# An absolute-sum normalization: summing and scaling of the first tile divided between two engines, 7 rows and 5

## The chip, the core and the metric

The kernel runs on one core of a Trainium2 chip. The engines that matter here are VectorE (DVE in the profile), ScalarE (ACT), SyncE (SP, which only issues transfers) and the core's 16 DMA engines, which move data between the chip's main memory (HBM) and the on-chip memory that the engines work on. The metric is device time in microseconds; the time of a kernel is the median of its runs.

## The reference

```python
# x: (32, 512, 1024) float32
def reference(x):
    sums = np.sum(np.abs(x), axis=-1, keepdims=True)
    return (x / (sums + 1e-8)).astype(np.float32)
```

Each of the 16384 rows of 1024 numbers is divided by the sum of its absolute values. 67.11 MB are read and 67.11 MB are written.

## The kernel before

The input is seen as 16384 rows. 128 partitions take part throughout, and each partition has 128 rows of its own. A tile is `[128, R, 1024]` with `R = 12` rows for each partition, so one tile is 6144 KB, and 49152 bytes of it lie in each partition. There are 11 tiles: the list `rows` holds ten times 12 and at the end 8. The first two tiles and the last one, of 8 rows, together make up the "head" of 32 rows a partition; `piece` says which rows of memory a tile covers. Its rows lie together in memory for each partition.

For each tile `i` in order the program does this:

- SP issues the load into `x_tile` (L78 before, L91 after the change). The pool `sbuf` has four buffers, so the first four loads are issued at once, and the load of tile `i + 4` is held on SP until the store of tile `i` has landed.
- `normalize` puts on DVE a sum of absolute values over all rows of the tile (`tensor_reduce`, L51, into `s`), an addition of 1e-8 (L58), a reciprocal (L60, into `inv`), and a product with `inv` in place for the first `kv` rows (L61). The remaining rows are scaled on ACT, one instruction a row (`activation` with `Copy` and a scale, L68). `kv` is `k - k // 3`: 8 of 12 rows are on DVE and 4 on ACT; in the last tile 6 and 2.
- ACT issues the store (L80), after its own rows and DVE's product are done.

All instructions of an engine run in the order in which the program puts them there (`manual_schedule`). So the store of a tile stands on ACT behind that tile's row copies, and the sum of the next tile stands on DVE behind the product of this one. Loads and stores use two separate queues, one fed by SP (q1 in the profile) and one fed by ACT (q10), on the same 16 DMA engines. One transfer is spread over all 16 engines, 8 partitions on each.

Of the kernel before, what the change touches and what calls it, by code (L numbers as in the profile page):

```python
# [1 line left out]

# [4 lines left out]

FP32 = mybir.dt.float32
EPS = 1e-8


@with_exitstack
def kernel(
    ctx: ExitStack,
    tc: tile.TileContext,
    x: bass.AP,
    out: bass.AP,
):
    nc = tc.nc
    P = nc.NUM_PARTITIONS  # L20

    x_flat = x.flatten_outer_dims()
    out_flat = out.flatten_outer_dims()
    n, d = x_flat.shape

    R = 12
    BUFS = 4  # L30
    HEAD = 32
    per_partition = n // P
    assert n % P == 0 and (per_partition - HEAD) % R == 0
    rows = [R] * ((per_partition - HEAD) // R + 2) + [HEAD - 2 * R]

    def piece(flat, i):
        head = flat[: P * HEAD, :].rearrange("(p r) d -> p r d", p=P)
        if i < 2:
            return head[:, R * i : R * (i + 1), :]
        if i == len(rows) - 1:  # L40
            return head[:, 2 * R :, :]
        a = P * (HEAD + R * (i - 2))
        return flat[a : a + P * R, :].rearrange("(p r) d -> p r d", p=P)

    sbuf = ctx.enter_context(tc.tile_pool(name="sbuf", bufs=BUFS))
    stats = ctx.enter_context(tc.tile_pool(name="stats", bufs=4))

    def normalize(x_tile, r0, k, kv):

        s = stats.tile([P, R], FP32)  # L50
        nc.vector.tensor_reduce(  # L51
            out=s[:, :k],
            in_=x_tile[:, r0 : r0 + k, :],
            axis=mybir.AxisListType.X,
            op=mybir.AluOpType.add,
            apply_absolute_value=True,
        )
        nc.vector.tensor_scalar_add(out=s[:, :k], in0=s[:, :k], scalar1=EPS)  # L58
        inv = stats.tile([P, R], FP32)
        nc.vector.reciprocal(out=inv[:, :k], in_=s[:, :k])  # L60
        nc.vector.tensor_mul(  # L61
            out=x_tile[:, r0 : r0 + kv, :],
            in0=x_tile[:, r0 : r0 + kv, :],
            in1=inv[:, :kv].unsqueeze(2).to_broadcast([P, kv, d]),
        )
        for r in range(kv, k):
            row = x_tile[:, r0 + r, :]
            nc.scalar.activation(  # L68
                out=row,
                in_=row,  # L70
                func=mybir.ActivationFunctionType.Copy,
                scale=inv[:, r : r + 1],
            )

    with tc.manual_schedule():
        for i, k in enumerate(rows):
            x_tile = sbuf.tile([P, R, d], FP32)
            nc.sync.dma_start(out=x_tile[:, :k, :], in_=piece(x_flat, i))  # L78
            normalize(x_tile, 0, k, k - k // 3)
            nc.scalar.dma_start(out=piece(out_flat, i), in_=x_tile[:, :k, :])  # L80


# [1 line left out]
_INS = ['x']  # L84
_OUTS = [((32, 512, 1024), 'float32')]


# [23 lines left out]
```

## Time and profile before

| | us |
|---|---|
| median of 7 runs | 317.62 |
| lowest and highest run | 317.0, 318.92 |
| the profiled run's own time | 318.92 |
| its span, first to last instruction | 317.3 |
| DVE busy | 235.8 (74%) |
| ACT busy | 46.1 (15%) |
| loads, q1 | 67.11 MB, 49.6% of 16 engines' span |
| stores, q10 | 67.11 MB, 48.9% |

The span is the time between the first and the last instruction of the profiled execution; the run's own time is 1.6 us longer. Busy time is the time in which an engine ran instructions. The share of a DMA queue is the time that its packets took, as a part of the span of all 16 DMA engines. A packet is here the part of a transfer that one engine moves in one piece: a partition's 49152 bytes, or 32768 bytes in the last tile. The records of the packets have for each its queue, start, duration and size. Times in the timeline count from the span's start.

### The profile page before, as it was taken

To read this page: it belongs to the slowest core of one execution; us is meant where nothing else is said; L and a number is where in the kernel's file an instruction comes from. 1 tells how busy PE (TensorE), PEld (TensorE's weight loads), DVE (VectorE), ACT (ScalarE), POOL (GpSimd) and SP (SyncE) were. 2 spreads that over 40 slices of the span, in tenths; PEclk is the share of its full clock that TensorE was granted. 3 is DMA by queue.
4 is the path that set the end of the run, shared out by engine and by line. 5 is a ranking of instruction groups with operands and counts; after the bars stand their busy time and mean duration, and the time that the engine had idled before them with its cause. 6 is when DMAs were issued, how large, how long until landed. Compare 5 with 4: busy or idle time off the path is not lost.

```text
span 317.3 us, 205 instructions
## 1 busy us (share of the span) xinstructions
DVE 235.8 (74%) x44; ACT 46.1 (15%) x43; POOL 0.2 (0%) x4
## 2 busy tenths in 40 slices
DVE  0079999999999599659928990997399469979400
ACT  0010402205005004000500140031005000502000
POOL 0000000000000000000000000000000000000000
DMA  8999999999999999999999999999999999999994
GB/s 335 459 397 483 409 384 403 421 471 403 465 421 403 483 403 428 465 403 452 434 403 471 409 440 446 409 465 421 403 466 421 428 432 459 403 463 421 415 426 202
DMA packets 3170, 134.23 MB, mean 423 GB/s; under 512 B 353, under 2 KB 353, under 8 KB 353
## 3 DMA queue, kind: packets, MB, share of 16 engines
q1 hardware_dynamic: 1584, 67.11, 49.6%
q10 hardware_dynamic: 1584, 67.11, 48.9%
q14 instruction: 2, 0.01, 0.0%
HBM read 67.11 MB, written 67.11 MB: 423 GB/s over the span
## 4 chain that ended last, share of the span: by engine, by line
another core or an unknown queue 36%; DMA 31%; DVE 26%; SPq 0%; issue 0%; DVEq 0%; ACTq 0%
DMA out_dram<-x_tile 16%; DMA x_tile<-in_x_dram 15%; DVE s L51 15%; DVE x_tile L61 10%; SPq L78 0%; DVE inv L60 0%; DVE s L58 0%; DVEq L60 0%; ACTq L80 0%
## 5 line engine op out<-in xcount | busy, mean ns | idle before, releaser
L51 DVE TENSOR_REDUCE s<-x_tile 128x12 f32<-128x12288 f32 (+1 forms) x11 | 138.2, 12562 | 59.6 <-DMA x_tile<-in_x_dram 59.6
L61 DVE TENSOR_TENSOR x_tile<-x_tile,inv 128x8192 f32<-128x8192 f32 (+1 forms) x11 | 93.5, 8498 | 0.4
L68 ACT ACTIVATE x_tile<-x_tile,inv 128x1024 f32<-128x1024 f32 x42 | 44.8, 1137 | 228.8 <-DVE inv L60 228.8
L68 ACT ACT_TABLE_LOAD x1 | 1.3, 1283 | 17.7 <-DMA x_tile<-in_x_dram 17.7
L60 DVE RECIPROCAL inv<-s 128x12 f32<-128x12 f32 (+1 forms) x11 | 2.5, 226 | 0.9
L58 DVE TENSOR_SCALAR s<-s 128x12 f32<-128x12 f32 (+1 forms) x11 | 1.9, 173 | 0.4
L95 POOL MEMSET const-bfloat16-1.0<- 128x1 bf16 x1 | 0.1, 101 | 0.0
L95 POOL MEMSET const-uint8-127<- 128x1 uint8 x1 | 0.1, 101 | 0.0
L95 POOL MEMSET const-float32-0.0<- 128x1 f32 x1 | 0.1, 98 | 0.2 <-issue 0.2
L95 POOL MEMSET const-float32-1.0<- 128x1 f32 x1 | 0.1, 98 | 0.0
## 6 DMA issues: line engine op xcount, KB each, us to landing
x_tile<-in_x_dram SPq DMA_DIRECT2D x10, 6144.0 KB, 34.2
out_dram<-x_tile ACTq DMA_DIRECT2D x10, 6144.0 KB, 52.5
x_tile<-in_x_dram SPq DMA_DIRECT2D x1, 4096.0 KB, 31.1
out_dram<-x_tile ACTq DMA_DIRECT2D x1, 4096.0 KB, 19.1
```

Source lines behind the costliest of these rows:

```text
L51: nc.vector.tensor_reduce(out=s[:, :k], in_=x_tile[:, r0 : r0 + k, :], axis=mybir.AxisListType.X, op=mybir.AluOpType.add, apply_absolute_v ...
L58: nc.vector.tensor_scalar_add(out=s[:, :k], in0=s[:, :k], scalar1=EPS)
L60: nc.vector.reciprocal(out=inv[:, :k], in_=s[:, :k])
L61: nc.vector.tensor_mul(out=x_tile[:, r0 : r0 + kv, :], in0=x_tile[:, r0 : r0 + kv, :], in1=inv[:, :kv].unsqueeze(2).to_broadcast([P, kv, d]),)
L68: nc.scalar.activation(out=row, in_=row, func=mybir.ActivationFunctionType.Copy, scale=inv[:, r : r + 1],)
L95: nc = _bacc.Bacc("TRN2", target_bir_lowering=False, num_devices=1)
```

## The change

`normalize` gets a further argument, `ks`: the sum on DVE covers the first `ks` rows, and ACT sums each of the other rows with an `activation` of the function `Abs` that also accumulates along the row into `s` (L65). What that instruction writes as its ordinary output goes to `junk`, a buffer in PSUM (the accumulation memory) that nobody reads. The addition of 1e-8 (now L71) then waits for DVE's sum and for ACT's. For tile 0 both `ks` and `kv` are 7 (of 12 rows), so that DVE sums and scales 7 rows and ACT sums and scales 5. For all other tiles `ks = k` and `kv = k - k // 3`, as before. The argument `r0`, which was always 0, is dropped. In the order of instructions nothing else moves, except that ACT's load of its function table stands ahead of the first wait for tile 0 instead of behind it.

```diff
+    psum = ctx.enter_context(
+        tc.tile_pool(name="psum", bufs=1, space=bass.MemoryType.PSUM)
+    )
+    junk = psum.tile([P, d], FP32)
+
-    def normalize(x_tile, r0, k, kv):
+    def normalize(x_tile, k, ks, kv):
         s = stats.tile([P, R], FP32)
         nc.vector.tensor_reduce(
-            out=s[:, :k],
-            in_=x_tile[:, r0 : r0 + k, :],
+            out=s[:, :ks],
+            in_=x_tile[:, :ks, :],
             axis=mybir.AxisListType.X,
             op=mybir.AluOpType.add,
             apply_absolute_value=True,
         )
+        for r in range(ks, k):
+            nc.scalar.activation(
+                out=junk[:, :],
+                in_=x_tile[:, r, :],
+                func=mybir.ActivationFunctionType.Abs,
+                accum_out=s[:, r : r + 1],
+            )
         nc.vector.tensor_scalar_add(out=s[:, :k], in0=s[:, :k], scalar1=EPS)
...
             nc.sync.dma_start(out=x_tile[:, :k, :], in_=piece(x_flat, i))
-            normalize(x_tile, 0, k, k - k // 3)
+            if i == 0:
+                normalize(x_tile, k, k * 7 // 12, k * 7 // 12)
+            else:
+                normalize(x_tile, k, k, k - k // 3)
             nc.scalar.dma_start(out=piece(out_flat, i), in_=x_tile[:, :k, :])
```

More of the change, by code (lines that the diff above doesn't have):

```diff
@@ L61, in normalize @@
         nc.vector.tensor_mul(
-            out=x_tile[:, r0 : r0 + kv, :],
-            in0=x_tile[:, r0 : r0 + kv, :],
+            out=x_tile[:, :kv, :],
+            in0=x_tile[:, :kv, :],
             in1=inv[:, :kv].unsqueeze(2).to_broadcast([P, kv, d]),
@@ L66, in normalize @@
         for r in range(kv, k):
-            row = x_tile[:, r0 + r, :]
+            row = x_tile[:, r, :]
             nc.scalar.activation(
```

## The prediction

> **What bounds the kernel now.** I read the page first, for the share of each resource.
>
> ```profile
> span 317.3 us, 205 instructions
> DVE 235.8 (74%) x44; ACT 46.1 (15%) x43; POOL 0.2 (0%) x4
> DMA  8999999999999999999999999999999999999994
> q1 hardware_dynamic: 1584, 67.11, 49.6%
> q10 hardware_dynamic: 1584, 67.11, 48.9%
> ```
>
> No engine is full, but the 16 DMA engines are: loads (q1) and stores (q10) together take 98.5% of the span, and only the first and the last slice lack a 9. Next I read busy time by stretches (columns: us, DVE, ACT, POOL, clock, DMA share, GB/s), cut where the first store begins and where the loads end.
>
> ```profile
> 1.70:42.00 40.30, 24.22 (x5) 5.55 (x5) 0.00 (x0) 1.00 1.01 429
> 46.00:276.00 230.00, 188.81 (x36) 38.39 (x36) 0.00 (x0) 1.00 1.00 432
> 281.00:302.00 21.00, 15.62 (x4) 2.19 (x2) 0.00 (x0) 1.00 1.02 440
> 302.00:313.00 11.00, 0.00 (x0) 0.00 (x0) 0.00 (x0) 1.00 0.92 399
> 313.00:317.30 4.30, 0.00 (x0) 0.00 (x0) 0.00 (x0) 1.00 0.05 23
> ```
>
> Loads alone, loads with stores, and stores alone all move 429 to 440 GB/s at a full DMA. The mixture is neither dearer nor cheaper, so an earlier mixture wins no bandwidth. The packet records say why: a 49152-byte packet takes 1.815 us on its engine in either queue, and a 32768-byte packet of the last tile 1.213 us. Each engine carries 8 packets of each transfer: 2 x (80 x 1.815 + 8 x 1.213) = 309.8 us. The records run from 1.73 to 315.86, 314.1 us. So 4.3 us at most is not plain transfer: 0.7 in the first packets, 1.2 where the first store joins, the rest on one late engine. Of the 16, 14 begin the last store at 303.2 to 304.1 and end by 313.8, one ends at 314.4, and the latest begins at 306.2 and ends at 315.9.
>
> The third view is the timeline, at both ends (start, duration, engine, line).
>
> ```profile
> 17.67 12.95 DVE L51 TENSOR_REDUCE s<-x_tile 128x12 f32<-128x12288 f32 x1 [17.67 <-DMA x_tile<-in_x_dram]
> 39.91 0.38 ACTq L80 DMA_DIRECT2D out_dram<-x_tile  x1
> 109.69 12.95 DVE L51 TENSOR_REDUCE s<-x_tile 128x12 f32<-128x12288 f32 x1 [3.70 <-DMA x_tile<-in_x_dram]
> 281.18 8.69 DVE L51 TENSOR_REDUCE s<-x_tile 128x8 f32<-128x8192 f32 x1 [2.03 <-DMA x_tile<-in_x_dram]
> 297.06 0.34 ACTq L80 DMA_DIRECT2D out_dram<-x_tile  x1
> ```
>
> The first store is issued at 39.91; from 109.69 on DVE waits for loads; the last load lands at 281.16 and the last store is issued 15.9 us later, at 297.06. The engines then still work on older stores until 303.2 or later. That cover, 6.1 us, is the number on which the change turns.
>
> **The change, part by part.** Tile 0 on DVE before: from 17.67 to 39.82, 22.15 us. After: its sum has 7 rows instead of 12. The forms of L51 give 12950 ns for 12 rows and 8686 for 8, so 1066 a row and 7.62 us for 7, a saving of 5.33. The product has 7 rows instead of 8: L61 gives 8692 ns for 8 rows and 6558 for 6, so 7.63 us, a saving of 1.07. In all 6.40 us.
>
> ACT gets five summing instructions. No row of before has one that accumulates. From below, the copies of L68 take 1137 ns and follow each other at 1067 (4.27 us for four), so five take 5.4 us. From above, I let each cost twice the copy, 2.27 us, for the wait of each on the one before and for bringing out the sum: 11.4 us. I take 1.3 us each, near the copy, the same 1024 elements in and out: 6.5 us, under DVE's 7.62. If that cover is gone, the add at L71, and the reciprocal and product queued behind it on DVE, start 3.8 us later, and the first store comes 2.6 us earlier instead of 6.4. ACT's fifth copy is hidden: 5 x 1.07 = 5.3 us beside a product of 7.63. The function-table load (1.28 us), which waited for the first load, no longer does and runs under it.
>
> One rule speaks against the change. The Trainium skill, "ScalarE: Activation LUTs", section "Rules for kernel authors", sends sums and products to VectorE rather than ScalarE; the trace has 1066 ns a row for DVE's sum and 1067 between ACT's copies, so a second engine is worth a second engine here. By the rule tile 0 would stay at 22.15 us, by the rows it falls to 15.75.
>
> So the first store is issued at about 33.5 instead of 39.9. DVE then finds tile 1 in place: loads alone need 8 x 1.815 = 14.5 us each, so the second lands at 17.65 + 14.5 = 32.2, before DVE is free at 33.4. Stores 1 to 8 stay queued ahead of need: before, store 0's packets begin at 45.2 and each store takes 29 us beside loads, while stores 1 and 2 are issued at 62.0 and 84.0. The fifth load, which SP holds until store 0 has landed, is issued some 6 us sooner, but queues behind the fourth.
>
> Now what the 6.4 us buy. The two queues alternate packet by packet. With the stores starting D earlier, D worth of load packets is pushed into the shared stretch, where each also waits for a store packet. So every later load, the last one too, lands D later, with D as much more store data done. The work left is the same. D is 6.4 us, in whole packets 5.4 (three) or 7.3 (four). The last landing moves to 287.6, and the last store's issue to 303.5 (302.5 to 304.3). DVE's wait before the last tile stays, as tile 9 moves along.
>
> The older stores still end at 303.2 to 304.1 on most engines, so the cover of the last store is used up. From issue to first packet the trace shows two cases: 1.0 us for the first load, on idle engines, whose first packets then take 0.7 longer, and 5.3 us for the first store (39.9 to 45.2) behind queued loads. The last store meets nearly empty queues, so I take 1.0 plus 0.7: data flows from 303.5 + 1.7 = 305.2 (304.2 to 306.0). The 14 engines, begun anew, end 8 x 1.213 = 9.7 us later, at 314.9 (313.9 to 315.7). The latest engine, busy until 306.2, is not held up and still ends at 315.9. Sum for the span: 0; I add 0.3 us because D, latency and lateness can only add up upward here.
>
> The Trainium skill, "DMA: Bandwidth & Descriptors", section "Specifications", gives about 0.6 us to the first byte of a transfer issued by sync or scalar; no idle-queue store in this trace shows it, and by it the sum for the span would also be 0.
>
> The profiled run took 318.92 us, its span 317.3 and 1.6 around it; the median is 317.62, 1.3 below. I carry the difference over: 317.62 + 0.3 = 317.9. About 0.3%, 0.95 us, is what a measurement of this kernel can tell from no change.
>
> **The rivals.** First, slower by a gap ahead of the last store. If issue to first packet costs more than 2.0 us (303.5 + 2.0 + 0.7 + 9.7 = 315.9), all engines stand idle and the gap sets the end. At the first store's 5.3 us, flow starts at 308.8 and ends at 318.5, +2.6; with four packets of shift at 319.3, +3.4: 320.2 to 321.0. Between, say 3.3 us, it is near +1.3 (318.9). For it: that 5.3 is the only store onto a queue that had been empty. Against it: those engines were full of loads. In unprofiled runs the latest engine may be less late, so the gap shows sooner, which favours this rival. Chance 0.27.
>
> Second, faster because the latest engine falls back into line. It lost 2.2 us in one packet where the first store joined (the others 1.2) and fractions of a microsecond in first packets of later loads. Another phase between the queues may spare it that: the end would then be 314.4, -1.5: 316.1. Against it: nothing in the change acts on that engine. Chance 0.11.
>
> Third, the full gain: tile 0's 6.4 us come off the end, 311.2. That would need the DMA to be idle somewhere for want of a store; the page and the stretches deny it. Chance 0.02.
>
> Fourth, it does not do what it says, ACT's sums being so slow that nothing is saved: tile 0 is then as before, 317.6, within my forecast's band.
>
> **How the numbers follow.** Forecast (no change that can be told) 0.60, slower 0.27, faster 0.13. The range leaves out the full gain, the far part of the second case and the top of the first: 316.5 to 320.0.
>
> **What would show it.** Right: first store issued near 33.5; add at L71 not waiting for ACT; last load landing 5 to 7.5 us later, near 287; last store issued near 303; the DMA full from 2 to 303. Wrong: the last landing not moved (then the queues do not alternate as I say), a hole of over 2 us in the stores after 303 (first rival), or a last packet that ends well before 315 (second rival).

## The result, and the profile after

The changed kernel has a median of 319.11 us in 31 runs (317.09 to 321.36), the kernel before one of 317.6 in 75 runs beside them. The ratio of the two is 1.0047, 95% interval 1.0033 to 1.0061: slower, by about half a per cent. The median hides what happens. The runs lie in two groups: 15 between 317.09 and 318.72, 16 between 319.11 and 321.36. Of the 75 runs of the kernel before only one is over 319, and of 95 more in the later rounds one. I call runs over 319 long and the others short. The median of the changed kernel is the lowest of its long runs: had one more of the 31 been short, it would have lain under 319. The profile that came with the result (run 320.5, span 318.7) is of a long run; a repeat of the same kernel gave the profile of a short one (run 317.43, span 315.7).

The page of the long run: ACT has taken over work, and the DMA's last two slices have thinned.

```profile
span 318.7 us, 216 instructions
DVE 229.6 (72%) x44; ACT 52.9 (17%) x54; POOL 0.2 (0%) x4
DMA  8999899999999999999999999999999999999966
q1 hardware_dynamic: 1584, 67.11, 49.4%
q10 hardware_dynamic: 1584, 67.11, 48.7%
```

The timeline of the same run (start, duration, engine, line) shows tile 0 and the end.

```profile
17.79 7.62 DVE L57 TENSOR_REDUCE s<-x_tile 128x7 f32<-128x7168 f32 x1 [17.79 <-DMA x_tile<-in_x_dram]
22.51 1.03 ACT L65 ACTIVATE junk<-x_tile 128x1024 f32<-128x1024 f32 x1
23.47 0.19 ACT L65 ACTIVATION_READ_ACCUMULATOR junk<-x_tile 128x1 f32 x1
25.52 0.17 DVE L71 TENSOR_SCALAR s<-s 128x12 f32<-128x12 f32 x1
25.99 7.62 DVE L74 TENSOR_TENSOR x_tile<-x_tile,inv 128x7168 f32<-128x7168 f32 x1
33.71 0.38 ACTq L98 DMA_DIRECT2D out_dram<-x_tile  x1
...
289.66 8.69 DVE L57 TENSOR_REDUCE s<-x_tile 128x8 f32<-128x8192 f32 x1 [2.13 <-DMA x_tile<-in_x_dram]
305.53 0.34 ACTq L98 DMA_DIRECT2D out_dram<-x_tile  x1
```

ACT's sums end at 23.7, under DVE's sum, and the first store is issued at 33.71 instead of 39.91. DVE has the last load at 289.66 instead of 281.18, and the last store is issued at 305.53. The short run of the same kernel has the same beginning (first store at 33.72) and another end:

```profile
286.57 8.69 DVE L57 TENSOR_REDUCE s<-x_tile 128x8 f32<-128x8192 f32 x1 [2.15 <-DMA x_tile<-in_x_dram]
...
302.44 0.34 ACTq L98 DMA_DIRECT2D out_dram<-x_tile  x1
```

Busy time by stretches (us, DVE, ACT, POOL, clock, DMA share, GB/s), first of the long run, then of the short:

```profile
46.00:276.00 230.00, 174.57 (x33) 34.13 (x32) 0.00 (x0) 1.00 1.00 433
302.00:313.00 11.00, 3.44 (x1) 0.00 (x0) 0.00 (x0) 1.00 0.73 314
313.00:318.70 5.70, 0.00 (x0) 0.00 (x0) 0.00 (x0) 1.00 0.44 190
```

```profile
46.00:276.00 230.00, 177.53 (x36) 34.41 (x33) 0.00 (x0) 1.00 1.00 433
302.00:313.00 11.00, 0.36 (x1) 0.00 (x0) 0.00 (x0) 1.00 0.92 399
313.00:315.70 2.70, 0.00 (x0) 0.00 (x0) 0.00 (x0) 1.00 0.00 0
```

The middle moves the same 433 GB/s in both; all the difference is in the end, where the long run has a hole (0.73) and a tail (0.44).

The packet records say what the tail is. They name no engine, but an engine begins its next packet within some 10 ns of the end of its last, so 16 chains of 176 packets can be followed. (Where two chains touch they can be exchanged; a lateness is then still real, but its early part may stand under a neighbour.) On 15 engines of the long run the older stores end at 303.4 to 304.8, the last store's packets begin at 306.4, 0.9 us after the issue, and end at 316.1 to 316.3. The sixteenth has no hole. It let the first store in after 19 load packets where the others had done 20, and from then on moves loads while they move stores. After 50 us its load packets lose 3.1 us in pieces of up to 0.67, and it ends at 317.09, 1.63 before the end of the span. So the hole, which the first rival had foretold, is there, but it did not set the time of this run: the latest engine did, by 0.8 us over the engines with the hole. The hole itself hangs on that engine, since the last load has landed only when the latest engine has moved its part.

### The profile page after: what moved, and what is told of

Same layout as the page of the kernel before. It is cut to its first block, busy times and chain, and to the rows that moved or that the text cites. A ratio compares the mean times of both kernels' runs of the same rounds, so it can differ in the third digit from the quotient of the medians.

```text
span 318.7 us, 216 instructions
## 1 busy us (share of the span) xinstructions
DVE 229.6 (72%) x44; ACT 52.9 (17%) x54; POOL 0.2 (0%) x4
## 4 chain that ended last, share of the span: by engine, by line
DMA 60%; DVE 31%; another core or an unknown queue 5%; issue 0%; DVEq 0%; SPq 0%; ACTq 0%
DMA x_tile<-in_x_dram 35%; DMA out_dram<-x_tile 25%; DVE s L57 17%; DVE x_tile L74 13%; DVE inv L73 0%; DVE s L71 0%; DVEq L73 0%; SPq L91 0%; ACTq L98 0%; DVEq L71 0%
## 5 line engine op out<-in xcount | busy, mean ns | idle before, releaser
L57 DVE TENSOR_REDUCE s<-x_tile 128x12 f32<-128x12288 f32 (+2 forms) x11 | 132.9, 12079 | 74.2 <-DMA x_tile<-in_x_dram 74.2
L74 DVE TENSOR_TENSOR x_tile<-x_tile,inv 128x8192 f32<-128x8192 f32 (+2 forms) x11 | 92.4, 8401 | 0.4
L81 ACT ACTIVATE x_tile<-x_tile,inv 128x1024 f32<-128x1024 f32 x43 | 45.9, 1136 | 231.5 <-DVE inv L73 231.5
L65 ACT ACTIVATE junk<-x_tile 128x1024 f32<-128x1024 f32 x5 | 5.1, 1027 | 15.9 <-DMA x_tile<-in_x_dram 15.8
L71 DVE TENSOR_SCALAR s<-s 128x12 f32<-128x12 f32 (+1 forms) x11 | 1.9, 172 | 0.5
L65 ACT ACTIVATION_READ_ACCUMULATOR junk<-x_tile 128x1 f32 x5 | 0.9, 186 | 0.0
```

The costliest lines, as they stand in the source:

```text
L57: nc.vector.tensor_reduce(out=s[:, :ks], in_=x_tile[:, :ks, :], axis=mybir.AxisListType.X, op=mybir.AluOpType.add, apply_absolute_value=True,)
L65: nc.scalar.activation(out=junk[:, :], in_=x_tile[:, r, :], func=mybir.ActivationFunctionType.Abs, accum_out=s[:, r : r + 1],)
L74: nc.vector.tensor_mul(out=x_tile[:, :kv, :], in0=x_tile[:, :kv, :], in1=inv[:, :kv].unsqueeze(2).to_broadcast([P, kv, d]),)
L81: nc.scalar.activation(out=row, in_=row, func=mybir.ActivationFunctionType.Copy, scale=inv[:, r : r + 1],)
```

## The experiments

Five theories stood against each other. A: the earlier first store moves the last load back, the last store loses its cover, and the hole sets the time. B: only the latest of the 16 engines counts. C, later E: dividing tile 0, or an earlier first store as such, costs the time. D, formed after the first four of these kernels had run: the phase decides, that is the place within the 1.815 us of a load packet at which the first store joins. F, against D: the delay as such counts.

**The changed kernel again.**

> The changed kernel once more, beside the others. Its 31 runs lie in two groups, about 317.1 to 317.7 and 319 to 321.4. Theory A (cover of the last store): where the profiled run is one of the shorter group, its last load lands by about 288 instead of 289.7, the last store is issued by about 304 and follows the older stores with a gap under 1 us; in the longer group the gap is about 3 us. Theory B (the latest of the 16 DMA engines alone): the gap is the same in both groups and only one engine's end differs. Median expected 317 to 320.5.

Median 317.37 in 12 runs, 4 of them long (320.58 to 321.54); ratio 1.0032, interval 0.9999 to 1.0066. In its short profile the last store is issued at 302.44, its packets begin near 303.6 with no hole, and the engines end at 313.1 to 314.0. Three engines are out of step there (19 load packets ahead of the first store, the rest 20) and lose 0.45 us at most after 50 us. So being out of step is not by itself being late, and the hole belongs to the long run alone; which of the two, hole or engine, makes a run long, this pair does not say.

**The first store held back.**

```diff
+            if i == 0:
+                for r in range(8):
+                    nc.scalar.activation(out=junk[:, :],
+                        in_=x_tile[:, 7 + r % 5, :],
+                        func=mybir.ActivationFunctionType.Copy)
             nc.scalar.dma_start(out=piece(out_flat, i), in_=x_tile[:, :k, :])
```

> The changed kernel with the first store held back: ACT runs 8 row copies into the unread buffer between its own rows of tile 0 and the first store, which is then issued near 40 as in the kernel before, while DVE still goes on to tile 1 at 33.5. Theory A (the first store's time moves the last load, and the last store loses its cover): the last load lands near 281 again, the last store is issued near 297, no gap, and the time is that of the kernel before, 317.6 within 0.3%, without the long group. Theory C (the divided sum itself, its PSUM writes or DVE's earlier start on tile 1 cost the time): the time stays that of the changed kernel, about 319 with runs up to 321.

First store at 38.44, last landing 280.90, last store at 296.78; 317.8 us, ratio 1.0014, interval 0.9998 to 1.0029; two of 12 runs are just over 319 (319.03 and 319.3), none over 320. The divided sum, its PSUM writes and DVE's early start on tile 1 are all still there. What the changed kernel loses hangs on the time of the first store; C falls.

**The last tile divided as well, and it alone.**

```diff
+            elif i == len(rows) - 1:
+                normalize(x_tile, k, 5, 5)
```

For the last tile alone this branch stands in place of the one for tile 0, which is then treated as in the kernel before.

> The changed kernel with the last tile divided too: DVE sums and scales 5 of its 8 rows, ACT 3. The chain from the last landing to the last store falls from 15.9 to 5 x 1.066 + 0.5 + 5.3 = 11.2 us. Theory A: the last load still lands 5 to 8.5 us later than before (286.5 to 289.7), but the last store is issued by 301, before the older stores are through at 303.5, so there is no gap; all runs near 317.1, the long group gone. Theory B (latest engine): the end does not depend on the last store's issue, two groups as before, median 317 to 320.

> The kernel before with only the last tile divided, 5 rows on DVE and 3 on ACT; tile 0 as before. Theory A: the last store had 6 us of cover already, so issuing it 4.7 us sooner (at 292.4) changes nothing: 317.6 within 0.3%. Theory C (dividing a tile between the engines costs time by itself): slower, by up to 1.5 us, as the changed kernel. A rival gain from a shorter end of the program would give 313.

With both tiles divided the last store is issued at 299.23, before the older ones are through, and the profile has no hole. Yet 3 of 12 runs are long (319.59, 320.94, 320.98); median 317.38, ratio 1.0014, interval 0.9984 to 1.0045. That profile is of a short run (318.46), so it does not show by itself that the long runs had no hole; a profile of a long run without one comes below (the kernel before with four more reciprocals), and with it A fails as their cause. With the last tile alone divided the last store is issued at 291.49, 5.6 us sooner than before, and the time does not fall: 317.86, ratio 1.0017, interval 1.0002 to 1.0033, one of 12 runs over 319 (319.64).

**The hole by itself.**

```diff
+            if i == len(rows) - 1:
+                twice = stats.tile([P, R], FP32)
+                nc.vector.tensor_reduce(out=twice[:, :k], in_=x_tile[:, :k, :],
+                    axis=mybir.AxisListType.X, op=mybir.AluOpType.add,
+                    apply_absolute_value=True)
             normalize(x_tile, 0, k, k - k // 3)
```

> The kernel before with the last tile's sum taken twice on DVE, 8.7 us more between the last landing and the last store, which is then issued at about 305.8 instead of 297.1 (as in the long profile of the changed kernel, 305.5). The older stores end at 303.2 to 304 on most engines, the last store's packets begin 0.9 us after issue, so 15 engines stand idle for about 3 us and end 9.8 us after 306.7, at 316.5. Theory A (the gap sets the end): all runs up by the gap less the latest engine's lateness, 318.0 to 320, no short runs. Theory B (only the latest engine counts): 317.6 as before.

Median 317.97, ratio 1.0021, interval 1.001 to 1.0033, no run over 318.5. The last landing came at 279.17 in this profile, so the last store was issued at 303.64 rather than 305.8. Fourteen engines stood idle, most of them for 0.8 to 1.5 us, and ended together at 314.2 to 314.4, where the median engine of the profile before ends at 313.2. A hole of about 1.2 us costs about half a microsecond and makes no long runs: A's mechanism is real, and small at this size. A hole of 3 us, as the expectation had it, did not come about and stays untested by itself.

**Shifting the first store.** A repeated reciprocal changes no value and takes about 0.26 us on DVE ahead of tile 0's product. Two, six and seven more of them were put into the changed kernel, four and seven into the kernel before.

```diff
-        nc.vector.reciprocal(out=inv[:, :k], in_=s[:, :k])
+        for _ in range(1 + extra):    # tile 0 only; 2, 6, 7 or 4, 7
+            nc.vector.reciprocal(out=inv[:, :k], in_=s[:, :k])
```

(The diff is shortened: `extra` is a further argument of `normalize`, 0 for all other tiles.)

> The changed kernel with tile 0's reciprocal repeated twice more, which only delays its first store by about 0.5 us, to 34.2. Theory D (phase): the first store joins about 1.6 us after its issue; the load packets of the 16 engines begin near 34.9 to 35.6 and then every 1.815 us; where the joining falls among those beginnings, some engines let the store in one packet sooner than the rest, run out of step, and the latest of them sets the end. At 34.2 + 1.6 = 35.8 it falls between two beginnings: no or one engine out of step, runs near 317.1, none over 319. Theory E (dividing the first tile, or any earlier first store, brings the long runs): 4 or 5 of 12 runs over 319, as in the changed kernel.

> The changed kernel with tile 0's reciprocal repeated six times more: the first store is issued about 1.5 us later, near 35.2, and joins near 36.8, in the midst of the next beginnings (36.7 to 37.4). Theory D: engines out of step again, and a group of runs over 319. Theory E: as the changed kernel, 4 or 5 of 12 runs over 319. With rec2 it separates the two: only by D do they differ.

> The kernel before, tile 0 undivided, with its reciprocal repeated four times more: the first store is issued about 1 us later, near 40.9, and joins near 42.5, in the midst of beginnings (42.3 to 42.8). Theory D: the long group of runs (over 319) turns up in the kernel before, some of 12 runs, median up to 319. Theory E, and the plain reading that a microsecond on the way to the first store costs nothing: 317.6 within 0.3%, at most one run over 319.

> The kernel before with tile 0's reciprocal repeated seven times more, which delays the first store by 1.8 us, a whole load packet (1.815 us), to about 41.7. Four times more (40.96) had brought 9 of 12 runs over 319. Theory D (phase): the phase is that of the kernel before again, so no run or one over 319 and a median of 317.6 within 0.3%. Theory F (any delay of the first store in this kernel costs): 320 or more, as with four.

> The changed kernel with seven more reciprocals: first store near 35.54, a whole packet after the changed kernel's 33.72. Theory D: the phase of the changed kernel, so some 3 to 6 of 12 runs over 319, although six more (35.28) had none. Theory F (the delay as such helps): none over 319, 317.25.

The first stores were issued as follows: the kernel before with four more and with seven more, then the changed kernel with two, six and seven more.

```profile
40.96 0.38 ACTq L81 DMA_DIRECT2D out_dram<-x_tile  x1
41.77 0.38 ACTq L81 DMA_DIRECT2D out_dram<-x_tile  x1
34.26 0.37 ACTq L99 DMA_DIRECT2D out_dram<-x_tile  x1
35.28 0.38 ACTq L99 DMA_DIRECT2D out_dram<-x_tile  x1
35.55 0.37 ACTq L99 DMA_DIRECT2D out_dram<-x_tile  x1
```

The number of load packets done when the first store is let in is counted for each of the 16 engines of one profile; those that differ from most are out of step, "early" with one packet fewer than most, "late" with one more. The rest is what remains of the time of issue after whole packets of 1.815 us.

| kernel | first store issued, us | rest, us | out of step, of 16 | long runs | ratio to before (95%) |
|---|---|---|---|---|---|
| before | 39.91 | 1.80 | 1 late | 1 of 75 | 1 |
| before, 4 more | 40.96 | 1.03 | 1 early | 9 of 12 | 1.0080 (1.0053 to 1.0107) |
| before, 7 more | 41.77 | 0.03 | 0 | 0 of 11 | 1.0008 (0.9996 to 1.0021) |
| changed | 33.71 | 1.04 | 1 early | 16 of 31 | 1.0047 (1.0033 to 1.0061) |
| changed, again | 33.72 | 1.05 | 3 early | 4 of 12 | 1.0032 (0.9999 to 1.0066) |
| changed, 2 more | 34.26 | 1.59 | 0 | 0 of 11 | 0.9999 (0.9988 to 1.0010) |
| changed, 6 more | 35.28 | 0.80 | 8, half | 0 of 12 | 1.0004 (0.9992 to 1.0016) |
| changed, 7 more | 35.55 | 1.07 | 3 early | 6 of 8 | 1.0061 (1.0035 to 1.0087) |
| changed, store held back | 38.44 | 0.33 | 3 late | 2 of 12 | 1.0014 (0.9998 to 1.0029) |
| both tiles divided | 33.76 | 1.09 | 2 early | 3 of 12 | 1.0014 (0.9984 to 1.0045) |
| last tile alone divided | 39.81 | 1.70 | 0 | 1 of 12 | 1.0017 (1.0002 to 1.0033) |
| last sum taken twice | 39.98 | 0.05 | 2 late | 0 of 11 | 1.0021 (1.0010 to 1.0033) |

This settles what the half per cent comes from. The undivided kernel, made one microsecond later at tile 0, becomes slower than the change made it; delayed by 1.86 us, about a whole load packet, it is as before. The divided kernel is as fast as before with its first store half a microsecond later, and slow again a whole packet later. Neither earlier nor later counts, nor divided or undivided: the place within the 1.8 us of a load packet does. E and F fall. The column of rests, worked out after all runs, says the same of every kernel: those with three or more long runs have rests of 1.03 to 1.09, divided or not, and no other kernel has its rest there.

One expectation of D was missed: with six more reciprocals half of the engines are out of step, and no run is long. The table says more nearly what long runs go with: wherever there are three or more of them, one to three engines were early in the profile, and late engines or an even split did not bring them. The three profiles of long runs have one, one and three engines out of step (changed, 4 more, changed with 7 more), and in each the latest engine is one of these, 0.8 to 4.3 us after the next. A lone late engine is not enough for a long run: in the short profiles of the kernel before (318.92) and of the changed kernel with two more (318.54) one engine in step ends 1.5 us or a little more after the next. The profile with six more has many slow packets (0.8 to 1.9 us lost on every engine after 50 us), but no engine far behind the rest (ends 314.1 to 315.5). All of this rests on one profile a kernel, two for the changed one.

The DMA's part of the profile from 302 to 320, in 40 slices, shows the lone engine to the eye. First the kernel before with four more reciprocals, then the changed kernel with two more:

```profile
DMA  2299389496891993989989911010010100100000
GB/s 109 109 437 619 146 364 655 182 728 291 364 765 73 437 655 146 655 364 437 437 364 437 655 73 73 0 73 0 0 73 0 73 0 0 73 0 0 0 0 0
```

```profile
DMA  9089999596895995968959951001000000000000
GB/s 546 0 364 437 401 437 437 218 728 291 364 655 218 583 437 218 728 291 364 655 218 583 437 218 73 0 0 73 0 0 0 0 0 0 0 0 0 0 0 0
```

A 73 is one 32768-byte packet beginning in a slice of 0.45 us: one engine at work. In the first the steady work ends after the 23rd slice and six lone packets follow, all but one of the latest engine, the last begun near 317.5; in the second, after the 24th, two. By the packet records the latest engine of the first ends at 318.68, all others by 314.4, and no engine stood idle ahead of its last store, which was issued in good time:

```profile
300.14 0.34 ACTq L81 DMA_DIRECT2D out_dram<-x_tile  x1
```

So here is a long run (321.73) without a hole: A is not needed for one, and B's latest engine sets its end.

**A version from the findings.** The changed kernel with two more reciprocals and the last tile divided too:

> A version made from the findings: the changed kernel with two more reciprocals on tile 0 (first store at 34.26, a phase without long runs) and with the last tile divided 5 rows to 3, so that the last store is issued before the older ones are through. No engine out of step, no gap: 317.0 to 317.3, no run over 319; against the kernel before 0.998 to 1.0, since the DMA engines' own work (309.8 us) is untouched.

317.59 us, a little above the 317.0 to 317.3 expected; ratio 1.0009, interval 0.9999 to 1.0018, no long run. Its profile has neither hole nor an engine out of step (the latest ends 0.8 us after the next), and it is not faster than the kernel before. In its profile the median engine ends at 313.3, in that of before at 313.2.

## Why the prediction was right or wrong

**The bound** was right: the DMA engines carry the same packets in the same 1.815 and 1.213 us, and the 6.2 us won on tile 0 (6.4 said) bought nothing. The middle stretch stayed full, and no kernel here beat the one before by what a measurement can tell.

**Tile 0** was right nearly to the number. DVE's sum and product took 7.62 each (7.62 and 7.63 said); ACT's five sums follow each other at 1.18, 5.9 in all (6.5 said), with a read of the accumulator of 0.19 after each; the add did not wait for them; the first store was issued at 33.71 (33.5).

**The shift of the last load** was right in kind. The median engine's last load packet ends at 281.9 in both profiles of the changed kernel against 276.3 before: 5.6 us, the three packets of the text, since the store enters after 20 load packets instead of 23. The Trainium skill, "DMA: Bandwidth & Descriptors", section "Queues, rings and completion order", says that a DMA engine goes round its queues packet by packet; the records agree, loads and stores taking turns at 1.815 us each. (At the end of each transfer a packet of 4 bytes takes its queue's turn on every engine, so the other queue then seems to go twice.) The landing itself waits for the latest engine, and moved by 5.4 us in the short run and by 8.5 in the long.

**The cover of the last store** was sized well: 0.9 us from issue to first packet (1.0 said; the 0.7 us of slow first packets did not come). The Trainium skill, "DMA: Bandwidth & Descriptors", section "Specifications", gives about 0.6 us to the first byte. The 0.9 count from the start of the issuing instruction; from its end, 0.34 us later, 0.5 to 0.65 remain, which agrees.

**The time** was 317.9 against 319.11, inside the range but in the part that the text gave to a rival, with a chance of 0.27 for slower against 0.60 for no change. That it lies inside the range is partly luck: 14 of the 31 runs are over its top of 320.0, and the median falls between two groups of nearly equal number. The step that failed is the one on the latest engine. "The latest engine, busy until 306.2, is not held up and still ends at 315.9" took its lateness as a constant that the change could only leave or lessen, and the second rival said that nothing in the change acts on that engine. The prediction also misread which engine that was. The engine that lost 2.2 us in one packet where the first store joined let the store in late, ends at 314.4 and loses nothing more after 50 us; the latest one, at 315.9, was in step and lost 2.4 us in later load packets. So lateness is no fixed property of an engine: it comes up on the way. The change moves the joining to another phase, and with it which engines fall out of step and how much they lose. After 50 us the latest engine lost 3.1 us in the changed kernel, 3.4 in the one with seven more reciprocals, and 4.7 in the undivided one with four more. (In the last the chain touches others from 134 to 139 us, but it is the same engine before and after: the second of its two stores in a row begins at 109.7, 139.5 and 169.4, where most others have theirs at about 106.8, 135.8 and 164.8.)

The first rival went to the right side by the wrong mechanism. It needed more than 2.0 us from issue to first packet, and 0.9 were measured; the hole came instead because the last landing, which waits for the latest engine, moved by 8.5 us in that run and not by 6.4, and a long run comes without it too.

**Still open** is why an early engine loses time in load packets in one run and hardly any in another of the same kernel, and why an even split does no harm. The records show the slow packets, not their cause.

## What to carry to other kernels

With the DMA full from end to end, moving work between compute engines changed only the order of the packets here, and the time was that of the latest of the 16 engines, not of their mean. This kernel lost up to 0.8% through the moment at which the second queue joined the first, and won nothing through the work saved. Before a small change is judged, shift that moment by a fraction of a packet and look at all runs rather than at the median. Where runs fall into two groups, take a profile of each.

## What the runs showed of the hardware

- A delay of about 1 us ahead of the first store made a kernel 0.8% slower (317.44 to 320.2), and one of about 1.9 us did not; a packet takes 1.815 us.
- Single load packets beside stores took up to 0.94 us longer than 1.815 in the profile before; the cause is not shown.
- An accumulating `activation` of 1024 elements took 1027 ns and a separate read of 186 ns; five followed each other at 1.18 us.
